# An attention-score product on one core: the stores of one late result, dealt out anew over the sixteen DMA engines

## The chip, the core and the metric

The kernel runs on one core of a Trainium2 chip. The metric is the device time of one execution in microseconds (us). The kernel before took 297.6 us in the median of three runs (297.45 to 297.6).

## The reference

```python
def setup_inputs():
    batch, n_heads, seq_t, seq_s, channels = 8, 12, 512, 512, 64
    return {
        "x": np.random.randn(batch, n_heads, seq_t, channels).astype(np.float32),
        "y": np.random.randn(batch, n_heads, seq_s, channels).astype(np.float32),
    }

def reference(x, y):
    return np.einsum('bhtc,bhsc->bhts', x, y).astype(np.float32)
```

There are 96 pairs of a batch and a head. For each, a 512x64 matrix is multiplied by the transpose of another, which gives 512x512 numbers. The inputs are 25.17 MB in all and the output is 100.66 MB, both float32, so four fifths of the traffic are stores.

## The kernel before

**Data.** Sixteen of the 96 matrices of x, or of y, make one load of 128 partitions by 4096 numbers (2048 KB), 12 loads in all. ACT, DVE and POOL turn them into bf16 and order them (`compress`, `mix`), DVE transposes them in blocks of 32 (`transposes`, L252 and L261), and PE multiplies (`products`, L275). There are 48 results, numbered 0 to 47; each is 128 partitions by 4096 float32 numbers, 2048 KB, written by PE into the two halves `pms[0]` and `pms[1]` of PSUM and copied by ACT (the last result by DVE) into one of eight slots of the SBUF buffer `room`. Two neighbouring slots make a pair. From result 6 on, two results are stored together by one DMA of 4096 KB from a pair, which SP issues at L188 (`transfer`).

**Order.** Every instruction is put into its engine's queue by a list written out by hand. `emit` keeps the last writer and the readers of each buffer and puts in the waits that follow from them. Four results share one set of transposed operands; `heads` gives the order in which these four are made. Results 44 to 47 are the last four, and result 44 is called `SHARED`.

**The last four results.** A partition of even number holds rows of the output's lower half (u = 0), one of odd number rows of the upper half (u = 1). For result 44 the 64 odd partitions, 16 KB each, 1024 KB in all, go out on their own in `shares` (L301):

- The DMA engines are dealt with by hand. A pair store of 64 partition pairs gives every one of the 16 engines the same bytes. A DMA whose outer dimension is 5, 3 or 8 is meant for as many engines. POOL issues such DMAs in the order of `turns` (L95): engines 0 to 4, then 5 to 7, then 8 to 15, twice, for b = 0 and b = 1; each engine gets two rows each time. For the first turn only the columns up to `CUT[b]` are taken, 512 and 1536 of 4096 (L313).
- SP issues two DMAs of four times two rows, for engines 0 to 3, that take the columns from `CUT[b]` on: 512 to 4096 for b = 0 and 1536 to 3072 for b = 1 (L315).
- What is left is remade: `again` (L330) lets PE compute the missing rows a second time, after all other products, so that they lie on other partitions; `rest` (L351) copies them by DVE into `xk0`, 96 partitions by 1024 numbers, and POOL stores them in three DMAs (L364) for engines 0 to 7, 8 to 12 and 13 to 15. The list `remade` (L320) says what: the fifth engine's rows of b = 0 in eighths, its rows of b = 1 in thirds, and the last 1024 columns of the first five engines' rows of b = 1 in fifths.

The even partitions of result 44 leave with those of 45 (L374), the odd ones of 45 by a store of their own (L378), and 46 and 47 by the last pair store (L387). At the end POOL waits for every semaphore and clears them (L457), in two steps, the last store's among the second.

Of the kernel before, what the change touches and what calls it, by code (L numbers as in the profile page):

```python
# [9 lines left out]
def kernel(  # L10
# [3 lines left out]
    y: bass.AP,  # L14
    out: bass.AP,
):

# [10 lines left out]
    _, _, S, _ = y.shape  # L30
    P = 128
# [10 lines left out]
    N = K * S  # L42
# [7 lines left out]
    while len(ROUNDS) < (V * NH - SINGLE) // 2:  # L50
        ROUNDS += [PAIRS - 1, *ROUND[LATE % 3:], *ROUND[:LATE % 3]]
    LAST = 2 * ROUNDS[(V * NH - SINGLE) // 2 - 1]
    CUT = [S, 3 * S]
    LEFT = 2 * S
    fp32 = mybir.dt.float32
    bf16 = mybir.dt.bfloat16
    u32 = mybir.dt.uint32
# [9 lines left out]
    def buffer(name, width, dtype):  # L67
        return nc.alloc_sbuf_tensor(name, [P, width], dtype)[:, :]
# [21 lines left out]
    xbs = [buffer(f"xb{half}", K * E * D, u32) for half in range(2)]  # L90
    xTs = [buffer(f"xT{i}", K * D * E, u32) for i in range(2)]
    yTs = [buffer(f"yT{i}", D * R // 2, u32) for i in range(2)]
    pms = [nc.alloc_psum_tensor(f"pm{i}", [P, 4, S], fp32)[:, :, :] for i in range(2)]

    turns = [(0, 5), (5, 3), (8, 8)]  # L95
    engines = {"act": nc.scalar, "dve": nc.vector, "pool": nc.gpsimd, "pe": nc.tensor, "sp": nc.sync}
# [3 lines left out]
    def need(name, points, told=True):  # L100

        best = {}
        for p, v in points:
            if known[name].get(p, 0) < v:
                best[p] = max(best.get(p, 0), v)
        for p, v in list(best.items()):
            if any(snaps[q, w].get(p, 0) >= v for q, w in best.items() if q != p):
                del best[p]
        for p, v in best.items():
            if told:  # L110
                engines[name].wait_ge(sems[p], v)  # L111
            known[name][p] = v
            for q, w in snaps[p, v].items():
                known[name][q] = max(known[name].get(q, 0), w)

    def promise(name, reads, writes):

        points = [writer[r] for r in (*reads, *writes) if r in writer]
        points += [v for w in writes for v in readers.get(w, ())]
        if name == "pool" and name in ticks:  # L120
            points.append((name, ticks[name]))
        return points

    def record(name, p, step, reads, writes, queue=False):
        at = (p, ticks.get(p, 0) + step)
        ticks[p] = at[1]
        if not queue:
            own[name][p] = at[1]
        snaps[at] = {**known[name], **own[name], p: at[1]}
        for r in reads:  # L130
            readers.setdefault(r, []).append(at)
        for w in writes:
            writer[w], readers[w] = at, []

    def signal(p):
        if p not in sems:
            sems[p] = nc.alloc_semaphore(p)
        return sems[p]

    def emit(name, make, reads=(), writes=(), dma=None, by=None, step=1):  # L140
        need(name, promise(name, reads, writes))
        p = by or name
        if dma is not None:
            p, step = f"dma{dma}", 16
        made = make().then_inc(signal(p), step)
        record(name, p, step, reads, writes, dma is not None)
        return made.ins.name
# [6 lines left out]

    places = [0, 4, 3, 1, 2, 0, 4, 3, 1, 2, 4, 3]
    first = [0, 1, 2, 4, 0, 1]
    heads = [0, 2, 1, 3]
    held = {
        SLOTS + g - 1: [[("xk", g)], [("yb", h, g, ch) for h in range(2) for ch in range(2)]]
        for g in spares  # L160
# [14 lines left out]
    def both(*ids):  # L175
        return [("slot", i, pm) for i in ids for pm in range(2)]

    def place(ap, pattern):
        name = ap.tensor.name
        return mybir.PhysicalAccessPattern(  # L180
            ap=pattern, offset=ap.offset, dtype=ap.dtype, memref=name, memsetref=f"{name}_set"
        )

    def transfer(name, dst, src, to=None, of=None):

        to = to or dst.ap
        of = of or [src.ap[0], *[[1, 1]] * (len(to) - len(src.ap)), *src.ap[1:]]
        return engines[name].add_instruction(  # L188
            mybir.InstDMACopy(
                name=nc.get_next_instruction_name(),  # L190
                engine=engines[name].engine,
                ins=[place(src, of)],
                outs=[place(dst, to)],
                mode="Copy",
                cce_op=mybir.AluOpType.bypass,
                queue={"sp": "qSPDynamicHW", "pool": "qPoolDynamic"}[name],
            )
        )
# [94 lines left out]
    def part(name, dst, src, k, reads, dma):  # L293

        assert src.ap[0][1] == 2 * k and dst.ap[0][1] == k
        emit(
            name, lambda: transfer(name, dst, src, dst.ap),
            reads=reads, dma=dma,
        )

    def shares(o, s):  # L301

        to, mine = ov[o // V, heads[o % V]], slots[s]
        def odd(name, b, e, k, lo, hi):

            p = 4 * e + 32 * b + (32 if e > 7 else 0)
            n = 2 * k
            dst = to[p // 2:p // 2 + n, 1, lo:hi].rearrange("(k i) n -> k i n", i=2)
            part(name, dst, mine[p + 1:p + 2 * n:2, lo:hi], k, both(s), "pool" if name == "pool" else s)

        for b in range(2):
            for e, k in turns:
                odd("pool", b, e, k, 0, N if e else CUT[b])  # L313
        for b in range(2):
            odd("sp", b, 0, 4, CUT[b], N - b * LEFT)  # L315

    remade = [  # L320
        (1, CUT[1], (N - LEFT - CUT[1]) // 3, 4, 13, 3, 0),
        (1, N - LEFT, LEFT, 20, 8, 5, 0),
        (0, CUT[0], (N - CUT[0]) // 8, 4, 0, 8, 0),
    ]

    def lies(e):
# [39 lines left out]
    def store(o):  # L366
        i, j = divmod(o, V)
        if o == SHARED:
            s = 2 * ROUNDS[(o - SINGLE) // 2]
            shares(o, s)  # L370
        elif o == SHARED + 1:
            n = ROUNDS[(o - SINGLE) // 2]
            emit(
                "sp", lambda: transfer("sp", ow[i, heads[j - 1]][:, :2], pairs[n][::2]),  # L374
                reads=both(2 * n, 2 * n + 1), dma=2 * n,
            )
            emit(
                "sp", lambda: transfer("sp", ov[i, heads[j]][:, 1], slots[2 * n + 1][1::2]),  # L378
                reads=both(2 * n + 1), dma=2 * n + 1,
            )  # L380
        elif o in ALONE:
            s = first[o]
            emit("sp", lambda: nc.sync.dma_start(ov[i, heads[j]], slots[s]), reads=both(s), dma=s)
        elif o % 2:
            n = first[o] // 2 if o < SINGLE else ROUNDS[(o - SINGLE) // 2]
            emit(
                "sp", lambda: transfer("sp", ow[i, heads[j - 1]], pairs[n]),  # L387
                reads=both(2 * n, 2 * n + 1), dma=2 * n,
            )
# [98 lines left out]
```

## Time and profile before

| | |
|---|---|
| median of three runs | 297.60 us |
| the profiled execution | 298.19 us |
| its span, first to last instruction | 296.36 us |
| busy, ACT / DVE / PE / POOL | 205.5 / 157.7 / 132.5 / 64.7 us |
| bytes moved by DMA, mean rate | 125.85 MB, 425 GB/s |
| POOL's queue (q0), packets and bytes | 384, 0.89 MB |
| pair stores of 4096 KB, median from issue to landing | 21, 23.3 us |

The page of the profile gives busy time by engine, the span in 40 slices with the busy share of the DMA engines in tenths, the DMA queues (q1 is SP's, q0 is POOL's), the chain of work that ended last, and the groups of instructions with their durations. The chain of waits follows the last instruction back to what released it. The table by stretches gives busy time and the DMA share of stretches of the span. The DMA view counts the packets that start in a stretch, by queue, and lists the DMAs by size. A packet is what one DMA engine moves in one go; the trace has its start, its duration, its queue and its bytes. Each of the 16 engines ends its part of a DMA with a packet of 4 bytes, here called its end mark, which raises the DMA's semaphore; the trace has that event too, here called the landing.

### The profile page before, as it was taken

The page shows a single profiled execution, that of the slowest core. Times are in us where ns is not written, and L with a number is a line of the kernel's source. Part 1 is how long each engine was busy: PE and PEld are TensorE (multiplying, and loading weights), DVE is VectorE, ACT ScalarE, POOL GpSimd, SP SyncE. Part 2 cuts the span into 40 slices and gives each one's busy share as a digit, 9 for nine tenths or more (in the row PEclk, how much of TensorE's full clock was granted, in tenths as well). Part 3 has the DMA queues.
Part 4 walks back from the last instruction along what each step waited for, and adds up shares of the span by engine and source line. Part 5 has one row for each costly group of instructions (what it writes and reads, how often), then busy time and mean ns, then how long its engine had stood idle before and what let it go on. Part 6 is the DMA issues. An engine that isn't in the chain of part 4 may idle for free.

```text
span 296.4 us, 1215 instructions
## 1 busy us (share of the span) xinstructions
PE 132.5 (45%) x397; PEld 36.5 (12%) x403; DVE 157.7 (53%) x76; ACT 205.5 (69%) x106; POOL 64.7 (22%) x33
## 2 busy tenths in 40 slices
PE   0000044434756455447555865546448655761000
PEld 0000011101211111111111211111111111121000
DVE  2167798896978681924908568772925100052000
ACT  1665669996999878667966999969666966640000
POOL 2399989997000000000000000000000000402000
PEclk9999999976799997897767699997895767677555
DMA  7999999999999999999999999999999999999996
GB/s 279 427 429 440 431 429 427 425 456 402 436 436 429 429 443 460 429 429 429 425 425 430 438 447 438 425 429 429 429 425 429 447 447 429 432 425 417 440 432 287
DMA packets 5898, 125.85 MB, mean 425 GB/s; under 512 B 936, under 2 KB 936, under 8 KB 980
## 3 DMA queue, kind: packets, MB, share of 16 engines
q1 hardware_dynamic: 5512, 124.95, 98.4%
q0 software_dynamic: 384, 0.89, 0.8%
q14 instruction: 2, 0.02, 0.0%
HBM read 25.17 MB, written 100.66 MB: 425 GB/s over the span
## 4 chain that ended last, share of the span: by engine, by line
DMA 59%; ACT 24%; PE 5%; issue 2%; DVE 1%; POOL 1%; SPq 0%; ACTq 0%
DMA out_dram<-room 46%; ACT room L167 22%; DMA room<-in_y_dram 7%; DMA room<-in_x_dram 6%; PE pm L275 4%; ACT xk L167 1%; PE pm L344 1%; DVE room L169 1%; POOL out_dram L188 1%; DVE xk L169 0%; SPq L204 0%; ACTq L111 0%
## 5 line engine op out<-in xcount | busy, mean ns | idle before, releaser
L167 ACT ACTIVATE room<-pm 128x2048 f32<-128x2048 f32 x94 | 170.2, 1891 | 37.2 <-DMA out_dram<-room 34.3
L275 PE MATMUL pm<-yT,xT 128*128 128x512 bf16 x378 | 129.5, 480 | 134.6 <-ACT room L167 96.6
L252 DVE STREAM_TRANSPOSE xT<-xb 128x2048 uint32<-128x2048 uint32 x12 | 46.7, 3889 | 59.7 <-PE pm L275 54.9
L275 PEld LDWEIGHTS pm<-yT,xT 128*128 128x128 bf16 x384 | 35.0, 112 | 228.7 <-ACT room L167 150.0
L188 POOL DMA_DIRECT2D out_dram<-room x6 | 3.5, 590 | 180.9 <-ACT room L167 180.9
L169 DVE COPY xb<-room 32x2048 bf16<-32x2048 bf16 x20 | 26.1, 1305 | 0.6
L167 ACT ACTIVATE room<-room 128x4096 bf16<-128x4096 f32 (+1 forms) x6 | 18.2, 3035 | 11.2 <-DMA room<-in_x_dram 7.3
L169 POOL COPY xb<-xk 32x2048 bf16<-32x2048 bf16 x8 | 23.6, 2948 | 6.9 <-ACT xk L167 6.5
L169 DVE CAST yb<-room 64x2048 bf16<-64x2048 f32 x6 | 17.1, 2857 | 9.6 <-DMA room<-in_y_dram 9.6
L169 DVE COPY room<-pm 128x2048 f32<-128x2048 f32 x2 | 4.5, 2285 | 31.9 <-PE pm L275 31.9
L169 DVE CAST room<-room 64x2048 bf16<-64x2048 f32 x6 | 19.1, 3179 | 4.1 <-DMA room<-in_y_dram 4.0
L169 DVE COPY xb<-xk 32x2048 bf16<-32x2048 bf16 x16 | 20.9, 1304 | 0.4
L167 ACT ACTIVATE xk<-room 128x4096 bf16<-128x4096 f32 x3 | 10.9, 3617 | 3.2 <-DMA room<-in_x_dram 3.2
L169 POOL CAST yb<-room 64x2048 bf16<-64x2048 f32 x4 | 12.7, 3173 | 0.5
L169 POOL COPY xb<-room 32x2048 bf16<-32x2048 bf16 x4 | 12.7, 3179 | 0.3
L261 DVE STREAM_TRANSPOSE yT<-yb 128x1024 uint32<-128x1024 uint32 x6 | 11.6, 1936 | 0.0
L261 DVE STREAM_TRANSPOSE yT<-room 128x1024 uint32<-128x1024 uint32 x6 | 11.5, 1919 | 0.0
L169 POOL CAST room<-room 64x2048 bf16<-64x2048 f32 x3 | 8.5, 2829 | 1.0 <-DMA room<-in_y_dram 0.7
L167 ACT ACTIVATE yb<-room 64x2048 bf16<-64x2048 f32 x2 | 4.9, 2459 | 1.3 <-DMA room<-in_y_dram 1.3
L188 POOL DMA_DIRECT2D out_dram<-xk x3 | 1.7, 572 | 13.1 <-DVE xk L169 13.1
L167 ACT ACT_TABLE_LOAD x1 | 1.3, 1283 | 4.2 <-PEq L420 4.2
L428 DVE MEMSET xb<- 128x2048 uint32 x1 | 1.8, 1765 | 4.6 <-PEq L420 4.6
(8 smaller groups left out, 7.8 us busy)
## 6 DMA issues: line engine op xcount, KB each, us to landing
out_dram<-room SPq DMA_DIRECT2D x21, 4096.0 KB, 23.3
room<-in_x_dram SPq DMA_DIRECT2D x6, 2048.0 KB, 17.9
room<-in_y_dram SPq DMA_DIRECT2D x6, 2048.0 KB, 20.8
out_dram<-room SPq DMA_DIRECT2D x5, 2048.0 KB, 12.1
out_dram<-room SPq DMA_DIRECT2D x1, 1024.0 KB, 29.4
out_dram<-room POOLq DMA_DIRECT2D x2, 256.0 KB, 18.4
out_dram<-room POOLq DMA_DIRECT2D x2, 96.0 KB, 16.4
out_dram<-room SPq DMA_DIRECT2D x1, 112.0 KB
```

The costliest lines, as they stand in the source:

```text
L167: lambda: nc.scalar.activation(dst, src, COPY)
L169: else engines[name].tensor_copy(dst, src),
L188: return engines[name].add_instruction(mybir.InstDMACopy(name=nc.get_next_instruction_name(), engine=engines[name].engine, ins=[place(src, ...
L252: lambda: nc.vector.transpose(xTs[half].rearrange("p (k r e) -> p k e r", k=K, e=E), xbs[half].rearrange("p (k e c) -> p k e c", k=K, e=E),),
L261: lambda: nc.vector.transpose(yTs[half].rearrange("p (r j) -> p j r", r=D), ybs[half][b].rearrange("p (j c) -> p j c", c=D),),
L275: last = nc.tensor.matmul(pms[k // 4][:, j, :], xT[:, k + j, h, :], yT[:, h * S:(h + 1) * S], start=True, stop=True,)
L344: last = nc.tensor.matmul(pms[0][:top, at // S, at % S:at % S + hi - lo], xT[:, stop - top:stop], yT[:, h * S + lo % S:h * S + lo % S + hi ...
L428: lambda: engines[name].memset(xbs[half], 0.0),
```

## The change

- POOL's two DMAs for engines 0 to 4 (512 and 1536 columns) are gone. In each one's place POOL copies 5 partitions of 128 numbers (512 bytes each) from `xb0` into a new buffer `passed`, a DMA inside SBUF.
- SP's two DMAs for engines 0 to 3 take all columns: 4096 for b = 0, and the first 3072 for b = 1.
- The fifth engine's rows are remade in full but for the last 1024 columns of b = 1, which are in fifths as before: eighths of 4096 columns (512 each, 448 before) and thirds of 3072 (1024 each, 512 before). The cuts fall on multiples of 512, so that 16 products take the place of 19.
- `heads` is [1, 3, 0, 2] and not [0, 2, 1, 3].

```diff
-    CUT = [S, 3 * S]
     LEFT = 2 * S
...
+    passed = buffer("passed", 2 * P, u32)
...
-    heads = [0, 2, 1, 3]
+    heads = [1, 3, 0, 2]
...
-        def odd(name, b, e, k, lo, hi):
+        def odd(name, b, e, k, hi=N):
             p = 4 * e + 32 * b + (32 if e > 7 else 0)
             n = 2 * k
-            dst = to[p // 2:p // 2 + n, 1, lo:hi].rearrange("(k i) n -> k i n", i=2)
-            part(name, dst, mine[p + 1:p + 2 * n:2, lo:hi], k, both(s), "pool" if name == "pool" else s)
+            dst = to[p // 2:p // 2 + n, 1, :hi].rearrange("(k i) n -> k i n", i=2)
+            part(name, dst, mine[p + 1:p + 2 * n:2, :hi], k, both(s), "pool" if name == "pool" else s)
         for b in range(2):
             for e, k in turns:
-                odd("pool", b, e, k, 0, N if e else CUT[b])
+                if e:
+                    odd("pool", b, e, k)
+                else:
+                    emit(
+                        "pool", lambda: transfer("pool", passed[:k, P * b:P * (b + 1)], xbs[0][:k, :P]),
+                        [("xb", 0, 0)], [("passed", b)], "pool",
+                    )
         for b in range(2):
-            odd("sp", b, 0, 4, CUT[b], N - b * LEFT)
+            odd("sp", b, 0, 4, N - b * LEFT)
...
     remade = [
-        (1, CUT[1], (N - LEFT - CUT[1]) // 3, 4, 13, 3, 0),
+        (1, 0, (N - LEFT) // 3, 4, 13, 3, 0),
         (1, N - LEFT, LEFT, 20, 8, 5, 0),
-        (0, CUT[0], (N - CUT[0]) // 8, 4, 0, 8, 0),
+        (0, 0, N // 8, 4, 0, 8, 0),
     ]
```

## The prediction

> **What bounds the kernel now.** I read the page first, for what is busy all the time.
>
> ```profile
> span 296.4 us, 1215 instructions
> ...
> DMA  7999999999999999999999999999999999999996
> ...
> HBM read 25.17 MB, written 100.66 MB: 425 GB/s over the span
> ...
> DMA 59%; ACT 24%; PE 5%; issue 2%; DVE 1%; POOL 1%; SPq 0%; ACTq 0%
> ```
>
> The DMA engines are full from the second slice to the last but one; ACT, the busiest compute engine, has 69%. So the time is 125.85 MB through 16 DMA engines, plus what the last slice loses. Next, the end of the chain of waits:
>
> ```profile
> 227.16 31.71 DMA out_dram<-room
> ...
> 258.96 1.89 ACT room L167
> ...
> 265.17 2.93 PE pm L344 x19
> ...
> 268.11 1.23 DVE xk L169
> ...
> 269.63 1.71 POOL out_dram L188 x3
> ```
>
> Nothing is computed after 271.3 us, 25 us ahead of the end; SP issued its last 4096 KB store at 267.3 us (timeline, L188). The rest is a backlog that 16 engines drain. So I cut the end into stretches:
>
> ```profile
> core 0: us, PE busy (x) PEld busy (x) DVE busy (x) ACT busy (x) POOL busy (x), PEclk, DMA share, GB/s
> 280.00:290.00 10.00, 0.00 (x0) 0.00 (x0) 0.00 (x0) 0.00 (x0) 0.00 (x0) 0.50 1.02 435
> 290.00:294.00 4.00, 0.00 (x0) 0.00 (x0) 0.00 (x0) 0.00 (x0) 0.00 (x0) 0.50 0.91 393
> 294.00:294.80 0.80, 0.00 (x0) 0.00 (x0) 0.00 (x0) 0.00 (x0) 0.00 (x0) 0.50 0.11 41
> ```
>
> A packet counts where it starts. After 294 us almost none starts; the DMA view of 294.30 to 296.40 us says how few:
>
> ```profile
> DMA packets 17, 0.03 MB, mean 16 GB/s; under 512 B 16, under 2 KB 16, under 8 KB 16
> ...
> q1 hardware_dynamic: 17, 0.03, 4.0%
> ```
>
> Sixteen end marks of 4 bytes, one for each engine, and a single 32 KB packet. **One engine is last, alone.** The trace's packet records (start, length, queue, bytes) date it: 15 engines end their last packet between 294.38 and 294.77 us, the sixteenth at 295.83. The landing events of that store say the same: 15 from 294.70 to 295.17, the last at 296.29, and the span ends at 296.36.
>
> Which engine? Between the last and the last but one landing of each 16-engine store the gap grows evenly, 0.20 us at 62.5 us, 1.27 at 150.9, 2.44 at 258.9, 2.60 at 269.3, though all engines carry equal bytes; then 1.61 at 279.4, 1.12 at 286.6, 1.13 at the end. It falls exactly while result 44's unequal shares pass. Five engines carry 6144-byte POOL packets (266.48 to 269.25 us); four of them mark the end of a pair store at 275.52, 275.68, 275.82 and 276.09 and at once begin 14,336-byte packets, SP's 4-engine store. The fifth has none, and its mark, at 278.73, is the last of the 16. So the late one is the **fifth engine** (number 4), the one that the shares already spare.
>
> **The change, part by part.** Shares of result 44's upper rows by engine, KB, from lines 303 to 324 (16 KB is a whole row; 4 rows each if equal):
>
> - Engines 0-3: before 56 (POOL 16, SP 40) + 3.5 remade = 59.5; after 56 (all SP) + 4 = 60, and 1 KB of copy.
> - Engine 4: before 16 + 3.5 = 19.5; after 0 + 4, and 1 KB of copy.
> - Engines 5-7: 67.5, after 68. Engines 8-12: 72 both times. Engines 13-15: 68, after 72.
>
> Both sums are 1024. Packet durations of before: 16,384 bytes 0.61 us, 6144 bytes 0.24, 4096 bytes 0.16 (two rows of 2048 join in one), 3584 bytes 0.14.
>
> *Engine 4* loses one 4096-byte packet (0.16) and two of 6144 (0.48), in all 0.64 us; its remade piece grows from 0.14 to 0.16; it gains two copy packets of 512 bytes. Before has none from SBUF to SBUF; the nearest rows are the 4-byte mark, 0.01 us, and the 4096-byte packet, 0.16, so two cost 0.02 to 0.32. I take 0.03 each, by size between them: 0.06. Sum: -0.64 + 0.02 + 0.06 = **-0.56 us** (-0.30 to -0.60).
>
> *Who is late next?* Engines 13-15 gain 4 KB: six packets of 4096 in place of three, one more each, +0.16. Followed by their 4096-byte packets at 283.32, 283.32 and 283.63 to the end, they finish at 294.45, 294.45 and 294.75; after that 294.91 at most. Engine 4 comes to 295.83 - 0.56 = 295.27, still last by 0.36. So the whole 0.56 reaches the end.
>
> *POOL* issues six DMAs for the shares in both (L188, 566 ns median). The first copy now waits for DVE's last write of its source (last mix of half 0, L169, from 192.88 us) and not for ACT: it goes out 58 us early, and behind it stand only the stores, which wait for ACT at 253 us anyway. One issue, 0.57 us, leaves the row there. SP issues the same five; its 4-engine stores grow from 112 and 48 KB to 128 and 96.
>
> *PE and DVE:* 16 remade products for 19 (2.93 us in the chain; at their median, 300 ns, three would be 0.9), and the same 96x1024 copy (1.22). Cost nothing: the remade stores landed at 284.8 us at the latest, and 11.5 us of backlog lay behind them. Without that cover the gain would be up to 0.9 us. *Order of heads* [1,3,0,2]: same stores, sizes and turns; only which head's 1 MB goes first. I take 0; bounds, from how far the three runs lie apart, +-0.15.
>
> The profiled execution took 298.19 us, 1.83 around its span of 296.36; the median of the runs is 297.60, 0.59 less. Profiled: 298.19 - 0.56 = 297.63. For the median I take the same difference: 297.60 - 0.56 = **297.04 us**, -0.19%. About 0.2% (0.6 us) is what a measurement of this kernel can tell from no change, so the forecast lies almost on that line, by a hair inside.
>
> [...] The trace's late engine is the fifth, and it is 1.08 us behind engines 13-15 (295.83 against 294.75) even with the smallest share. [...]
>
> **Rivals.**
>
> 1. *The copy does not move the turn (slower).* POOL's 5, 3 and 8 engines follow one another only if a transfer of five partitions takes five engines and leaves the next to start at the sixth. For stores of 5x2 rows the trace bears it out: the late engine is among their five. No copy of shape 5x128 inside SBUF is in it. If the turn stood still, POOL's parts would fall on engines 0-2 and 3-10, 11-13 and 14, 15, 0-5, and the remade ones on 6-13, 14-2 and 3-5: engine 4 would carry 72 KB, engines 0-3 56 + 72 = 128. At 0.61 us for 16 KB engine 4 gains 52.5 KB, +2.0 us, to 297.8; engines 0-3 68.5 KB, +2.6, to 297.4 at most. The end moves by +2.0: 299.6 us. It decides as soon as the copy shifts the turn by anything but five. [...]
>
> 2. *Without the profiler the late engine is less late.* The profile's execution is 0.59 us longer than the median. If all of that lay in engine 4, its lead would be 1.06 - 0.59 = 0.47, and the others, +0.16 at most, would end first after a gain of 0.3; if it were not late at all, engines 13-15 would make it +0.16. Against: nothing says that the profiler costs just there. 297.1 to 297.76.
>
> 3. *Relief worth more than its bytes.* Engine 4 alternates between POOL's and SP's packets in the stretch where it falls behind, and each change of queue may cost it. The cap is where another engine is last: 296.29 - (295.17 + 0.16) = 0.96 us, so 296.64. Against: it falls behind as evenly before, without POOL packets.
>
> **How the numbers follow.** Forecast, engine 4 relieved by its bytes and still last: 0.62, its own range 296.8 to 297.3 by the copies' bounds, the heads and the runs' spread; about 0.30 of it beyond 0.2%, 0.32 within. Rival 1: 0.15, slower. Rival 2: 0.13, within. Rival 3: 0.07, faster. Heads or the copies in some other way slower: 0.03. Faster 0.37, same 0.45, slower 0.18. The range takes in all but rival 1 and this last: 296.7 to 297.8.
>
> **What would show it.** Right: the last landing gap is about 0.57 to 0.7 (1.13 before), in the DMA view of the end still one 32 KB packet beside 16 marks, last landing near 295.7; five 512-byte packets near 194 us and five more near 254; POOL's 16,384-byte packets in groups of three and eight as before. Rival 1: marks of the last store spread over 3 us, several 32 KB packets after 295 us. Rival 2: the gap falls in the profile, the median does not follow. Rival 3: the gap is near zero. The forecast is wrong if the gap at 258.9 us, ahead of the shares, is no longer 2.4: then the lateness is not a property of that engine.

## The result and the profile after

The changed kernel takes **300.13 us** in the median of six runs (300.03 to 300.37); the kernel before took 297.55 beside it (297.43 to 297.95). The ratio is 1.0086, with a 95% interval of 1.0073 to 1.0099: 2.58 us slower, where 0.56 us faster was forecast. The profiled execution took 300.37 us. Its page:

```profile
span 298.5 us, 1209 instructions
...
DMA  7999999999999999999999999999999999999996
GB/s 283 422 437 437 426 422 430 435 432 422 435 432 459 426 427 426 439 443 435 430 421 427 430 448 435 435 422 426 430 448 439 426 426 421 417 385 406 405 442 277
...
HBM read 25.17 MB, written 100.66 MB: 421 GB/s over the span
```

The DMA engines are as full as before, and move the same bytes, but from the 35th to the 38th slice, about 254 to 284 us, at 385 to 417 GB/s. Full engines at a lower rate: the packets last longer there. The stretches say it again; the last columns are the granted clock, the DMA share and GB/s. After, and then before, whose share is as full:

```profile
257.00:281.00 24.00, 7.26 (x25) 2.32 (x24) 5.71 (x3) 3.65 (x2) 1.66 (x3) 0.72 0.99 391
```

```profile
257.00:281.00 24.00, 6.89 (x31) 2.47 (x28) 5.71 (x3) 3.65 (x2) 1.71 (x3) 0.71 1.00 428
```

The DMA view of 294.3 us to the end, where before had 17 packets, one of them of 32 KB:

```profile
DMA packets 36, 0.66 MB, mean 139 GB/s; under 512 B 16, under 2 KB 16, under 8 KB 16
...
q1 hardware_dynamic: 36, 0.66, 32.5%
```

Sixteen end marks again, but twenty packets of 32 KB: not one engine is late, several are. By the packet records six engines begin their last 32 KB packet after 296 us and end it between 297.25 and 298.11. The end of the chain of waits has not moved much, and was over 27 us ahead of the end:

```profile
264.17 3.77 PE pm L351 x16
...
267.96 1.23 DVE xk L170
...
269.48 1.66 POOL out_dram L189 x3
```

**Which engines took which packets.** The packet records do not name the engine, but from 256 us on they can be strung into 16 chains in which each packet begins within 0.02 us of the end of the one before. A chain is taken here for an engine, and the engines' numbers are the layout's. Where two chains have an end at the same moment they can be mixed up. In the kernel before POOL's first three stores lie on sixteen different chains: the five-engine store on five (4096-byte packets from 257.81 to 258.86 us), the three-engine store on three others (16 KB packets from 261.20 to 261.40) and the eight-engine store on the eight that are left (264.88 to 265.38).

In the changed kernel POOL's first 16 KB packets, the three-engine store of b = 0, begin at 257.69, 257.96 and 258.11 us. The same three chains carry packets of 512 bytes, the second copy, at 266.91, 267.01 and 267.02. That copy's other two packets, at 265.10 and 265.91, are on chains that carry packets of the eight-engine store of b = 0, from 260.18 and 261.33. So the copy shares its five engines with the three-engine store and the first two of the eight-engine store. By the layout these are engines 0 to 4: the three-engine store meant for engines 5 to 7 fell on 0 to 2, and the eight-engine store began at engine 3, so the turn had not moved. This is how the prediction's first rival laid them out: engines 0 to 2 then take four of POOL's whole rows each, and the three chains do carry four packets of 16 KB each (257.69 to 258.11, 260.23 to 260.34, 271.80 to 271.91, 273.89 to 273.95).

### The profile page after: what moved, and what is told of

Read it like the earlier page. It is cut to its first block, busy times and chain, and to the rows that moved or that the text cites. A ratio compares the mean times of both kernels' runs of the same rounds, so it can differ in the third digit from the quotient of the medians.

```text
span 298.5 us, 1209 instructions
## 1 busy us (share of the span) xinstructions
PE 136.9 (46%) x394; PEld 37.0 (12%) x400; DVE 157.7 (53%) x76; ACT 205.3 (69%) x106; POOL 65.0 (22%) x33
## 4 chain that ended last, share of the span: by engine, by line
DMA 47%; ACT 18%; POOL 10%; DVE 10%; PE 4%; issue 3%; ACTq 0%; POOLq 0%
DMA out_dram<-room 40%; ACT room L168 17%; DVE room L170 5%; POOL xb L170 5%; DMA room<-in_y_dram 4%; POOL yb L170 3%; DMA room<-in_x_dram 3%; PE pm L276 2%; DVE xb L170 1%; DVE xT L253 1%; PE pm L351 1%; DVE yT L262 1%; ACT xk L168 1%; POOL room L170 1%; POOL out_dram L189 1%
## 5 line engine op out<-in xcount | busy, mean ns | idle before, releaser
L276 PE MATMUL pm<-yT,xT 128*128 128x512 bf16 x378 | 133.1, 493 | 130.8 <-ACT room L168 93.0
L189 POOL DMA_DIRECT2D passed<-xb x2 | 1.7, 844 | 121.8 <-DVE xb L170 121.8
L189 POOL DMA_DIRECT2D out_dram<-room x4 | 2.2, 564 | 57.6 <-ACT room L168 57.6
```

The source lines that it names most:

```text
L189: return engines[name].add_instruction(mybir.InstDMACopy(name=nc.get_next_instruction_name(), engine=engines[name].engine, ins=[place(src, ...
L276: last = nc.tensor.matmul(pms[k // 4][:, j, :], xT[:, k + j, h, :], yT[:, h * S:(h + 1) * S], start=True, stop=True,)
```

## The experiments

Ratios are to the kernel before, run beside each on the same chip, with 95% intervals.

**Is the copy the cause?** Four kernels were run together. The first puts real stores back into the copies' place, small ones; it is the kernel before with

```diff
-    CUT = [S, 3 * S]
+    CUT = [P, P + 64]
...
-    heads = [0, 2, 1, 3]
+    heads = [1, 3, 0, 2]
```

> The changed kernel with stores back in the place of the two copies: POOL's first turn stores 128 columns (b = 0) and 192 columns (b = 1) of the first five engines' rows, SP and the remade products take the rest; order of heads as changed. Theory (a copy inside SBUF does not move POOL's turn, a store does): the turns are right again, engine 4 carries 2.5 KB of POOL's rows and about 3.9 remade in place of 19.5, so 13.1 KB or 0.5 us less: 297.05 us, last landing gap 0.6. Rival (the copies did move the turn; the 2.6 us come from the whole rows on SP, the heads, or the remade products): these are still there, so 299.5 to 300.2.

Measured: 298.59 us, 1.0027 (1.0017 to 1.0038). Neither theory's number. No packet was misplaced: of the 44 packets of 16 KB in POOL's queue none took over 0.65 us, and engine 4 was no longer the last. Another engine was, one of 8 to 12: it carries 4096-byte packets of the five-engine remade store (281.58 and 282.95 us), and ended at 296.45 where all others ended by 294.87, but for one at 295.24, its last packet but one. On its chain two 32 KB packets took 1.65 and 1.61 us (from 267.68 and 270.26) and not 1.22, and between them lies a packet of 16 KB, from 269.33, that belongs to neither SP nor POOL:

```profile
q8 instruction: 1, 0.02, 0.0%
```

The kernel before has no such row; its only instruction packets are two of 8 KB in another queue, q14, at 106 and 162 us, and the runs have these too. The small cuts had made 28 remade products out of 19, so the guess was that PE's longer program needs another fetch. Two of the later kernels test that.

The second kernel adds the copies to the kernel before:

```diff
+    passed = buffer("passed", 2 * P, u32)
...
         for b in range(2):
             for e, k in turns:
+                if not e:
+                    emit(
+                        "pool", lambda: transfer("pool", passed[:k, P * b:P * (b + 1)], xbs[0][:k, :P]),
+                        [("xb", 0, 0)], [("passed", b)], "pool",
+                    )
                 odd("pool", b, e, k, 0, N if e else CUT[b])
```

> The kernel before with the two copies added, each ahead of POOL's five-engine store, and nothing else changed. Theory (the copies leave the turn where it is): as before, 297.55 us, within 0.2. Rival (they move it by five): every later store of POOL falls five engines further, engine 4 gets two whole pairs of rows (64 KB) for 16 KB and engines 0 and 1 as many beside SP's 40 KB, so about 1.7 us more: 299.2.

Measured: 297.62 us, 1.0 (0.9991 to 1.0009). None of the 44 packets of 16 KB took over 0.63 us. The copies do not move the turn.

The third takes the copies out of the changed kernel:

```diff
-    passed = buffer("passed", 2 * P, u32)
...
             for e, k in turns:
                 if e:
                     odd("pool", b, e, k)
-                else:
-                    emit(
-                        "pool", lambda: transfer("pool", passed[:k, P * b:P * (b + 1)], xbs[0][:k, :P]),
-                        [("xb", 0, 0)], [("passed", b)], "pool",
-                    )
```

> The changed kernel with the two copies left out and nothing in their place. Theory: they did nothing for the turn, so 300.1 us as the changed kernel, within 0.3, with the same engines late. Rival (they moved the turn, and the loss is elsewhere): without them the three- and eight-engine stores fall on engines 0 to 10 first, another 2 us: 302.

Measured: 300.08 us, 1.0076 (1.006 to 1.0091). With or without them the kernel is the same, which is the theory from the other side.

The fourth changes only the order of heads in the kernel before (`heads = [1, 3, 0, 2]`).

> The kernel before with the order of heads [1, 3, 0, 2] and nothing else. Theory: 297.55 us within 0.2; the gap at the last landing ahead of the shares (2.44 us before, 1.62 in the changed kernel) shows whether the order of heads makes engine 4 less late. Rival (the order of heads changes the stores' rate and is part of the 2.6 us): 298 or more.

Measured: 297.53 us, 0.9994 (0.9985 to 1.0004); the gap ahead of the shares was 2.15 us. The heads are innocent. But the gap at the last landing was 0.67, and in the run with copies 0.25, where the prediction's trace had 1.13: how late the last engine is differs from one execution to the next.

**Why does the copy not move the turn?** Two theories were left: its destination, or its form. This kernel keeps the destination and gives the copy the form of POOL's stores:

```diff
-    passed = buffer("passed", 2 * P, u32)
+    passed = buffer("passed", 4 * P, u32)
...
-                        "pool", lambda: transfer("pool", passed[:k, P * b:P * (b + 1)], xbs[0][:k, :P]),
+                        "pool", lambda: transfer(
+                            "pool", passed[:k, 2 * P * b:2 * P * (b + 1)].rearrange("p (i n) -> p i n", i=2)[:, :, :P // 2],
+                            xbs[0][:2 * k, :P // 2],
+                        ),
```

> The changed kernel with the two copies in the form of POOL's stores: the destination is still in SBUF, but as 5 partitions of two runs of 64 numbers, from 10 partitions of 64, in place of 5 times 128 from 5 times 128. Nothing else changes; 16 remade products. Theory A (what keeps the turn in place is the plain form, as many partitions on both sides): the turn moves by five, engine 4 is relieved by its 0.56 us, and 297.0 us, last landing gap under 0.7. Theory B (any transfer into SBUF leaves the turn in place): 300.1 us as the changed kernel, the same engines late.

Measured: 297.34 us, 0.9989 (0.998 to 0.9998). Theory A: the turn moves. The end of its DMA view, from 294.3 us, has no 32 KB packet left:

```profile
DMA packets 16, 0.00 MB, mean 0 GB/s; under 512 B 16, under 2 KB 16, under 8 KB 16
```

Its last landing gap is 0.12 us: no engine is late alone. The gain over the kernel before beside it (297.58) is 0.24 us and not 0.56.

The other way round, the plain form with a destination in DRAM, for POOL's two five-engine stores in the kernel before. It leaves out the second row of each pair in these columns, 40 KB of the output:

```diff
-                odd("pool", b, e, k, 0, N if e else CUT[b])
+                if e:
+                    odd("pool", b, e, k, 0, N)
+                else:
+                    row = 16 * b
+                    part(
+                        "pool", to[row:row + 2 * k, 1, :CUT[b]].rearrange("(k i) n -> k i n", i=2)[:, 0],
+                        mine[2 * row + 1:2 * row + 4 * k:4, :CUT[b]], k, both(s), "pool",
+                    )
```

> The kernel before with POOL's two five-engine stores in the copy's plain form, 5 partitions to 5 rows of the output; the second row of each pair of the first five engines is left out in these 512 and 1536 columns, 40 KB in all. Theory A (the plain form keeps the turn in place, wherever the data goes): POOL's stores fall as in the changed kernel, packets of 16 KB that take over 1 us, and about 299.8 us. Theory B (only a transfer into SBUF keeps it): the turns are as before and each of the first five engines has 8 KB less, 297.2 us.

Measured: 300.29 us, 1.0087 (1.0071 to 1.0102), with less to store; 23 of the 44 packets of 16 KB took over 0.7 us. So it is the **form**: 5 partitions to 5 rows left the turn where it was, into SBUF (300.13 us) or DRAM (300.29); 10 partitions to 5 times two rows moved it by five, into SBUF (297.34) or DRAM (the kernel before, 297.55). Whether the plain shape or the number of partitions decides was not tried, and why the form does so the runs do not show.

**The extra fetch.** The kernel before, with the last remade product done nine times more:

```diff
+        for _ in range(9):
+            last = nc.tensor.matmul(
+                pms[0][:top, at // S, at % S:at % S + hi - lo],
+                xT[:, stop - top:stop],
+                yT[:, h * S + lo % S:h * S + lo % S + hi - lo], start=True, stop=True,
+            )
         return last
```

> The kernel before with 28 remade products in place of 19: the last one is done nine times more, into the same place. Theory (beyond some length PE's program needs one more fetch of 16 KB, which one DMA engine makes while it stores, as the run with small stores showed at 269 us): one instruction packet on a queue of its own near 269 us, the two 32 KB packets beside it 0.4 us longer each, that engine 1.5 us late at the end, 298.2 to 298.6 us. Rival (the products only lengthen a chain that the backlog covers, and the loss of the run with small stores lies in its 128- and 192-column stores): 297.55 us.

Measured: 298.53 us, 1.0028 (1.0018 to 1.0039). The DMA view of 268 to 273 us (queue, packets, MB, share of 16 engines) has the fetch:

```profile
q1 hardware_dynamic: 66, 2.13, 100.6%
q0 software_dynamic: 63, 0.06, 3.3%
q8 instruction: 1, 0.02, 1.2%
```

It starts at 270.33 and takes 0.94 us; the 32 KB packets beside it took 1.70 and 1.60. Only PE instructions were added, and the kernel before has no such packet, so the fetch is taken to be for PE's program. The fetch and the two longer packets add 0.94 + 0.48 + 0.38 = 1.80 us on one engine, and one engine alone is that late: it ends at 296.25, the next at 295.23 and the others by 294.82. The remade stores are issued 1.1 us later (from 270.73 and not 269.63), which the backlog covers. So nine products that compute nothing new cost 0.95 us, because the engine that fetches them then sets the end.

The run with small stores again, with other cuts and so 24 products:

```diff
-    CUT = [P, P + 64]
+    CUT = [64, 768]
...
-        (1, CUT[1], (N - LEFT - CUT[1]) // 3, 4, 13, 3, 0),
+        (1, CUT[1], (N - LEFT - CUT[1]) // 3, 4, 13, 3, 256),
```

> As the run with small stores, but POOL's first turn takes 64 columns (b = 0) and 768 columns (b = 1), which the remade products can follow with 24 in place of 28. Engine 4 carries 6.5 KB of POOL's rows and 3.9 remade, 9.1 KB less than before, 0.35 us. If 24 products stay below the length that needs another fetch: 297.2 us and no instruction packet near 269 us. If not: 298.2 to 298.6 us with one.

Measured: 297.31 us, 0.9994 (0.9984 to 1.0003), no instruction packet after 161 us, last landing gap 0.17. With 24 products the fetch is not there, and with 28 it is, in two kernels of different cuts. So the first kernel's 1 us was the fetch.

**Why 2.6 us and not 2.0?** The kernel before with equal bytes on every engine, but rows of another engine's share on engines 8 to 15; the control has `(8, 4), (12, 4)` in that order:

```diff
-    turns = [(0, 5), (5, 3), (8, 8)]
+    turns = [(0, 5), (5, 3), (12, 4), (8, 4)]
```

> The kernel before, with each of POOL's two eight-engine stores split into two of four engines and these two in swapped order, so that engines 8 to 11 store the rows of 12 to 15 and the other way round. Every engine carries the bytes it had. Theory (an engine that reads rows which lie in another engine's share of the partitions slows both, as in the changed kernel, where 16 KB packets took up to 1.4 us and 32 KB packets up to 1.9): the same lengthening on engines 8 to 15 alone, four such packets each, 0.3 to 0.6 us apiece, so 1 to 2 us more: 298.5 to 299.5. Rival (only bytes count; the packets of the changed kernel are long because the engines were overloaded): 297.6 us, packets of 16 KB 0.61 us.

> The control for it: the same split into fours, in the order in which every engine stores its own share's rows. Both theories: 297.6 us, packets of 16 KB 0.61 us.

Measured: 300.64 us swapped, 1.0104 (1.0086 to 1.0122), and 297.54 in place, 1.0 (0.999 to 1.001). POOL's queue from 257 to 285 us, swapped and then in place (packets, MB, share):

```profile
q0 software_dynamic: 408, 0.83, 10.1%
```

```profile
q0 software_dynamic: 440, 0.87, 8.1%
```

Fewer bytes take more of the engines' time. Of the 44 packets of 16 KB, 20 took over 0.7 us and up to 1.52 when swapped; in place none took over 0.62. Of the 32 KB packets 21 took over 1.4 us, up to 1.90, close to 1.22 and 0.61 added. The theory had the size too small, 1 to 2 us where 3.1 were measured, but the place right. By the end marks of the last store eight engines are done at 294.44 to 295.10, as all 16 of the control are (294.48 to 295.08); four end at 297.08 to 297.30 and four at 298.08 to 298.28. These eight carry the remade packets of 4096 bytes that are meant for engines 8 to 15 (287.01 to 290.86 us). So at equal bytes the swap alone slows the engines whose rows were swapped, and no others. It changes the partitions that an engine reads and the output rows that it writes together; which of the two it is was not tried.

## Why the prediction was wrong, point by point

- **What bounds the kernel: right.** Every result came out of what the 16 engines do in the last 30 us, and none out of how long ACT, PE or DVE compute: the 16 remade products took 3.77 us, longer than the 2.93 of the 19, and nothing came of it.
- **Which engine was late: right for the trace that was read. That relief moves the end: right, but barely seen.** With the mended copies the ratio is 0.9989, just clear of no change; with small stores and 24 products, 0.9994, it is not clear. The small landing gaps of these two runs (0.12 and 0.17 us) prove nothing alone, since the control with the fours in place, which relieves no engine, has 0.04.
- **The step that failed** is the one behind the shares by engine: "after 56 (all SP) + 4 = 60, and 1 KB of copy" for engines 0-3 and "after 0 + 4" for engine 4 hold only if the copy takes five engines' turn. It does not: the shares came out as the rival's 128 KB and 72 KB, and the end moved by +2.58 us where -0.56 was summed. The copy's form alone turns this round, from 300.13 to 297.34 us. The prediction saw this as its first rival, with the layout as it came, named that no copy of this form was in the trace, and gave it 0.15. The evidence for the turn came from stores of 5x2 rows alone, and the copy differs from them in the one thing that counts.
- **The rival's price: mis-sized.** 2.0 us by bytes at 0.61 us for 16 KB; 2.58 were measured from median to median, and 2.18 from one profiled execution to the other (298.19 to 300.37), since the profile of before lay 0.59 above its median. The term left out is that a misplaced packet is also slow: 24 of the 44 packets of 16 KB took over 0.7 us in the changed kernel, up to 1.40, and 30 of the 32 KB packets over 1.4. The rival had engine 4 last, at 297.8, and engines 0 to 3 at 297.4 at most. But the four engines that carry the 12,288-byte packets of SP's four-engine store, engines 0 to 3, end at 297.77, 297.79, 297.82 and, last of all, 298.11. On the chain of engines 0 to 2 that begins at 258.11 the four packets of 16 KB took 1.01, 0.61, 0.78 and 0.79 us, 0.75 more than four times 0.61. The last to end is by its order of packets the odd one of the four, so most likely engine 3; how much of its 0.7 us beyond 297.4 is slow packets the records do not tell.
- **The size of the gain, had the turn moved: under half.** 0.24 us with the mended copies. The 1.13 us of lateness was that of one profiled execution, 298.19 us against a median of 297.60. Executions with the same shares had 0.04 (the fours in place), 0.25 (the kernel with copies) and 0.67 (the heads). Ahead of the shares the gap was 2.44 us in the prediction's trace, 1.62 in the changed kernel and 1.41 to 2.15 in the ten runs. By the prediction's own last sign the lateness is then no fixed property of that engine. This is the second rival, though not through the profiler: the lateness itself varies, why stays open, and where it is small there is less to gain by relief.
- **POOL's issue, SP's stores, the heads: nothing, as said.** The first copy was issued at 193.72 us. The heads alone measure 297.53.

## What to carry to other kernels

A filler that should stand for a transfer should have the transfer's form, not only its outer count of five (300.13 us here without it, 297.34 with it): look up in the trace on which engines the next packets land before anything is built on it. Where the DMA engines are full to the end, count everything that one of them does alone, an instruction fetch too (0.95 us here). And take the lateness of an engine from several executions (0.04 to 1.13 us here) before it is spent as a gain.

## What the runs showed of the hardware

- After a DMA of POOL from 5 partitions to 5 rows the next DMA began at the same engine as without it (300.13 us with such copies, 300.08 without); 10 partitions to 5x2 rows moved the start by five (297.34). The second copy's data lay on engines 0 to 4 (packets from 265.10 to 267.02 us), though by the layout the stores ahead of it had used engines 0 to 10.
- With the rows of engines 8 to 11 and 12 to 15 swapped (partitions and output rows both), at equal bytes, these eight were slowed: 16 KB packets went from 0.61 to as much as 1.52 us, 32 KB packets from 1.22 to 1.90, and the eight ended 2.0 to 3.8 us later while the other eight ended as before.
- With 24 remade products no instruction packet came after 161 us; with 28, in two kernels, there was one more, of 16 KB, near 270 us. It took 0.93 to 0.94 us of one DMA engine, and the two packets beside it took 0.38 to 0.48 us more each. With the DMA engines full it was 0.95 us of the kernel's time (298.53 against 297.58).
